# Low halves of the weights made on VectorE where norms run, in one step of a hybrid streaming encoder

## The chip, the core and the metric

The kernel runs on one core of one Trainium2 chip. The metric is the time of the program on the device in microseconds (us), the median of several runs. Besides the time there is a profile of one execution. The engines are called as in the profile: PE is TensorE (matmuls; PEld its weight loads), DVE is VectorE, ACT is ScalarE, POOL is GpSimd, SP is SyncE, which here issues the loads.

## What is computed

One layer of an encoder, for 512 tokens of a new stream and 8 x 16 tokens of running streams, 640 tokens of width 1024 in all, kept as five tiles of 128 tokens (tile 4 is the running streams). Cut to what matters:

```python
def encoder_layer(x, lw, ..., mem_k, mem_v):
    h = rmsnorm(x, lw['norm_mix'])
    a_qkv, b_qkv, b_beta, b_dec, b_gate, c_z, c_xbc, c_dt, gates = split_cols(h @ lw['w_in'], IN_SPLITS)
    ...
    m = ga * (ya @ lw['w_br_a']) + gb * (yb @ lw['w_br_b']) + gc * (yc @ lw['w_br_c'])
    x = x + m @ lw['w_out']
    x = x + memory_attn(rmsnorm(x, lw['norm_x']), mem_k, mem_v, lw['wx_q'], lw['wx_o'])
    hf = rmsnorm(x, lw['norm_ffn'])
    u, gf = jnp.split(hf @ lw['w_up'], 2, axis=-1)
    gf, f_conv_new = causal_dwconv(gf, f_conv, lw['f_conv_w'], lw['f_conv_b'])
    x = x + (u * jax.nn.silu(gf)) @ lw['w_down']
    return x, (...)

def memory_kv(mem, g, wk, wv):          # 256 memory rows, for the new stream
    m = rmsnorm(mem, g)
    return (m @ wk).reshape(...), (m @ wv).reshape(...)
```

`ya`, `yb` and `yc` come from three token mixers (chunk-band attention, gated DeltaNet, Mamba-2) that stand between the first projection and `w_out`; the change touches none of them.

## The kernel before

All matmuls are in a split float form. Each operand is held as a high half and a low half, both of type fp32r, and a product is three matmuls: high x high, low x high, high x low. For the activations a helper `split` (L258) makes the pair: ACT copies the value into the high half (line L250 of the profile), and another engine subtracts the high half from the value to get the low half (`tt`, L244). For weights `split_w` (L305) does the same on a block of 128 x 512 elements:

```python
            self.act(h[:, :m, :], x)
            eng = engs[b // half] if engs else self.nc.gpsimd
            ins = self.tt(l[:, :m, :], x, h[:, :m, :].bitcast(F32), ALU.subtract, eng)
```

So a low half of weights is made on POOL unless `engs` names an engine for the first and the second block of a loaded buffer. In the profile these instructions are `wl<-raw,wh` at L244, on POOL or on DVE. `raw` (L299) loads 512 KB of weights on the SP queue into one of 2 buffers, which are free again when both blocks' lows are made; high and low blocks have `NW = 6` buffers each, free again when PE has used them.

The work of the program is an in-order list for each engine. Which instruction stands where in a list is set by a scheduler when the program is built, from the order of the code and its own estimates; at run time an engine takes its list from the top, and an instruction that waits holds up all that stand behind it on its engine.

The norms are made in a chain that crosses the engines (`norm_T`, L519). ACT sums the squares of a token tile (`junk`); DVE turns the sums into a scale by some 14 tiny instructions of 128x1 or 128x2 elements (`inv_rms`, L487: names `v`, `y`, `w`, `t`); DVE multiplies the tile by scale and gain (`xn`, two instructions of 128x512 for each token tile, L247); PE transposes `xn` into PSUM (`nps`, L241); ACT copies the high half from there (`xTh`, `cTh`, `fTh`, `mTh`), and DVE makes the low half (`xTl` and so on). PE then multiplies these by weights.

Four stages run such chains while weights are split:

- **The front** (from 0 to some 45 us): tile 0, then tiles 1 and 2, then 3 and 4 are normed, and the attention values `V` (`tm`) are multiplied with four blocks of `w_in` from `rawv` and four from `raw`. The lows of the four `rawv` blocks are made at L1851 on POOL.
- **`w_out`** (955 to 1010 us): `add_proj` (L1520, called at L1933) goes through the 1024 columns in quarters of 256. A quarter loads two buffers, splits them in four blocks, and multiplies token tiles in pairs (0,1), (2,3), (4) (`ap<-wh,mh`); DVE adds the sums to `x`. All 16 lows are made on POOL. Between the quarters the norm of the memory (`mem_norm`, L1541) is run, two tiles of 128 rows (`mx`, `mT`).
- **Memory keys and values** (1010 to 1080 us): `mem_kv` (L1576) multiplies the normed memory by `wx_k` and `wx_v`, 8 steps of 256 columns with two buffers each (`tm<-wh,mTh`), woven with the norm of `x` for the cross attention (`cT`). Of the 32 lows, 16 are made on POOL and 16 on DVE.
- **The output of the cross attention** (1257 to 1298 us): `wx_o` is applied in the units `WP` (tiles 0 to 3, three quarters, earlier), `WL` (L1980: last quarter, all tiles) and `WS` (L1981: tile 4, three quarters). `WL` and `WS` split 16 blocks, 8 on POOL and 8 on DVE (`both`, L1962). The norm of the feed-forward (`fT`) runs beside them: tiles 0 and 1, tiles 2 and 3, and tile 4 when `WS` is done; then the feed-forward starts (`fps`, `ups`), whose lows are made on POOL.

Of the kernel before, what the change touches and what calls it, by code (L numbers as in the profile page):

```python
# [18 lines left out]
NK = 8  # L19
# [16 lines left out]
QUARTERS = ((0, 256), (256, 256), (512, 256), (768, 256))  # L36
# [9 lines left out]
class Enc:  # L46
# [1190 lines left out]
    def gates(self, X, gcol, tgs, mts):  # L1237
        w = self.I["w_in"][0]
        for mt in mts:
            def run(ps):  # L1240
                tg = tgs[mt] = self.U("tg")
                self.act(tg.rearrange("p (a b) -> p a b", a=2), ps[:, :, :HALF], AF.Tanh, scale=0.5)
            yield from self.fmj(lambda: self.weights(w, gcol + mt * P, P, 0, NK), X, run, nm="gps")

    def branch(self, X, Y, wbr, gcol, tgs, first):

        ahead = max(len(tgs), 1)
        yield from self.gates(X, gcol, tgs, range(len(tgs), ahead))
        Y = Y()
        nk = len(Y)  # L1250
        for mt in range(NK):
            yield from self.gates(X, gcol, tgs, range(mt + ahead, min(mt + ahead + 1, NK)))

            def run(ps):
                tg = tgs.pop(mt)
                tv = tg.rearrange("p (a b) -> p a b", a=2)
                self.stt(tv, tv, 1.0, ps[:, :, :HALF], ALU.add, ALU.mult)
                if first:
                    self.m.append(tg)
                else:  # L1260
                    self.tt(self.m[mt], self.m[mt], tg, ALU.add)
            if nk == 8:
                wk, c = (lambda: self.weights(wbr, mt * P, P, 0, 8)), 0
            else:
                if mt % 2 == 0:
                    pair = self.weights(wbr, mt * P, 256, 0, nk)
                wk, c = pair, (mt % 2) * P
            yield from self.fmj(wk, Y, run, c=c, nm="pps")
# [307 lines left out]
    def mem_kv(self):  # L1576
        I, O = self.I, self.O
        res = []
        for name, w in (("mem_k_prompt", I["wx_k"][0]), ("mem_v_prompt", I["wx_v"][0])):
            T = [[self.U("mkv", shape=(P, 512)) for _ in range(2)] for _ in range(2)]  # L1580
            res.append(T)
            dst = O[name][0, 0].rearrange("s h d -> s (h d)")
            for c in range(4):
                def cb(pair, ps):
                    for j, t in enumerate(pair):
                        self.act(T[t][c // 2][:, (c % 2) * 256:(c % 2) * 256 + 256], ps[:, j, :256])
                        if c % 2:
                            x = T[t][c // 2]
                            self.store(dst[t * P:(t + 1) * P, (c // 2) * 512:(c // 2 + 1) * 512], x)
                            if name == "mem_v_prompt":  # L1590
                                T[t][c // 2] = [self.U("mv", F32R, (P, 512)) for _ in range(2)]
                                self.split(*T[t][c // 2], x, self.nc.gpsimd)
                yield from self.tmj(lambda: self.weights(w, c * 256, 256, 0, NK, (self.nc.gpsimd, self.nc.vector)), self.MX, cb, tiles=range(2))
            if w is I["wx_v"]:
                break
            if len(res) == 1:
                K = T
                self.KT = []
        for h in range(4):
            pt = self.PP("mkt")  # L1600
            for dd in range(2):
                f = 2 * h + dd
                for kt in range(2):
                    self.tr(pt[:, dd * 256 + kt * P:dd * 256 + (kt + 1) * P],
                            K[kt][f // 4][:, (f % 4) * P:(f % 4 + 1) * P])
            o = [self.U("mKT", F32R, (P, 512)) for _ in range(2)]
            self.split(*o, pt)
            self.KT.append(o)
        self.MV = res[1]
# [211 lines left out]
    def run(self):  # L1821
        I = self.I
# [3 lines left out]
        w = I["w_in"][0]  # L1826
# [15 lines left out]
        for c, t in ((0, 1), (1, 3)):  # L1842
            if c == 0:
                tile0 = self.last_act
                for a in range(2):
                    wv += self.split_w(raws[a], 2, 512, loose=True)
            else:
                with self.tc.issue_after(tile0.ins):
                    for r in rawv:
                        h, l = (self.wp.tile([P, 512], F32R, name=self.nm("w" + b), tag="w" + b) for b in "hl")  # L1850
                        self.split(h, l, r, self.nc.gpsimd)  # L1851
                        wv.append((h, l))
            all_(self.norm_T(x0, g, X, ((t, t + 1),)))
        X = X[1]
# [69 lines left out]
        M = []  # L1924
        for mt in range(NK):
            h, l = self.U("mh", F32R), self.U("ml", F32R)
            self.act(h, self.m[mt], scale=0.5)
            self.stt(l, self.m[mt], 0.5, h.bitcast(F32), ALU.mult, ALU.subtract)
            M.append((h, l))
        x = [self.load_x(t) for t in range(NT)]  # L1930
        mem = self.mem_norm()
        next(mem)
        for i, _ in enumerate(self.add_proj(I["w_out"][0], M, x, cols=QUARTERS)):  # L1933
            if i % 10 == 9:
                next(mem, None)
        all_(mem)
# [4 lines left out]
        _, X = to  # L1941
# [16 lines left out]
        _, OX = self.XT("ox")  # L1958
        OS = [[self.U("os" + a, F32R, (P, 4, P)) for _ in range(2)] for a in "hl"]
        OS = [(OS[0][k // 4][:, k % 4, :], OS[1][k // 4][:, k % 4, :]) for k in range(NK)]  # L1960
        S = {}
        both = (self.nc.gpsimd, self.nc.vector)  # L1962
        self.add("WP", self.add_proj(I["wx_o"][0], OX, x, tiles=range(4), cols=QUARTERS[:3]), after=("XP",))
        cur = None
        for i in range(12):
# [19 lines left out]
        _, X = to  # L1985
# [53 lines left out]
```

## Time and profile before

| what | before |
|---|---|
| time, median of 3 runs | 1771.53 us (1765.14, 1771.53, 1771.67) |
| the profiled execution's own time | 1764.74 us |
| its span, first to last instruction | 1763.0 us |
| mean granted clock of TensorE, share of full speed | 0.985 |
| chain that ended last, PE's and DVE's shares | 69% and 11% of the span |
| moved by DMA | 181.78 MB, mean 103 GB/s |

The profiled execution took 1.7 us beyond its span, and 6.8 us less than the median of the runs. A row of the timeline reads: start, duration, engine, line, operation, output<-inputs, shapes, count, and in brackets how long the engine was idle before it and what ended that. Where a row has a count above one, the duration is that of the whole run of instructions.

### The profile page before, as it was taken

How to read it: one execution, taken by the hardware profiler on the slowest of the kernel's cores; microseconds unless marked ns; L12 is line 12 of the kernel's file. 1: busy time of each engine (PE TensorE's matmuls, PEld its weight loads, DVE VectorE, ACT ScalarE, POOL GpSimd, SP SyncE). 2: the span in 40 equal slices, each digit the busy share in tenths (PEclk: the TensorE clock that was granted, in tenths of full speed). 3: DMA queues.
4: the chain of work that ended last, by engine and by line, in shares of the span. 5: the costliest groups of instructions: out<-in, count | busy, mean ns of one | idle time of the engine just before them, and what ended most of it. 6: DMA issues, size and time to landing. Idle time of an engine off the chain costs nothing.

```text
span 1763.0 us, 32520 instructions
## 1 busy us (share of the span) xinstructions
PE 1678.3 (95%) x12953; PEld 1539.4 (87%) x12953; DVE 867.3 (49%) x1762; ACT 650.0 (37%) x1596; POOL 610.2 (35%) x641
## 2 busy tenths in 40 slices
PE   7999999999999998999999899999889999999997
PEld 5887778898988898998899899987689989998996
DVE  6155762437777764756434472243564404431443
ACT  4234544324443432443342354342443313331332
POOL 3342221123332343453432335211143433433432
PEclk8999999999999999999999999999999999999999
DMA  6322166222232334335323345146332222222221
GB/s 191 100 74 61 43 197 209 93 82 79 54 81 77 98 108 114 86 101 145 85 61 119 109 131 179 49 168 239 121 96 78 80 72 78 79 73 79 77 86 72
DMA packets 232830, 181.78 MB, mean 103 GB/s; under 512 B 14401, under 2 KB 198726, under 8 KB 232550
## 3 DMA queue, kind: packets, MB, share of 16 engines
q1 hardware_dynamic: 210752, 165.74, 30.8%
q10 hardware_dynamic: 21926, 13.96, 2.6%
q8 instruction: 102, 1.67, 0.4%
q14 instruction: 50, 0.41, 0.1%
HBM read 163.09 MB, written 16.06 MB: 102 GB/s over the span
## 4 chain that ended last, share of the span: by engine, by line
PE 69%; DVE 11%; ACT 3%; DMA 3%; issue 2%; POOL 1%; ACTq 0%; SPq 0%; POOLq 0%; DVEq 0%
PE ups L236 9%; PE fps L236 9%; PE dn L236 8%; PE gps L236 8%; PE pps L236 6%; PE ap L236 5%; PE tm L236 5%; PE qps L236 3%; PE cps L236 2%; DVE xc L247 2%; PE bps L236 2%; PE pl L236 1%; DVE t L244 1%; PE py L236 1%; PE t5a L241 1%
## 5 line engine op out<-in xcount | busy, mean ns | idle before, releaser
L244 POOL TENSOR_TENSOR wl<-raw,wh 128x512 fp32r<-128x512 f32 x369 | 489.2, 1330 | 940.6 <-ACT wh L250 770.9
L250 ACT ACTIVATE wh<-raw 128x512 fp32r<-128x512 f32 x396 | 246.5, 629 | 567.5 <-PE fps L236 92.9
L247 DVE SCALAR_TENSOR_TENSOR xc<-xp,vec,xc 128x664 f32<-128x664 f32 (+1 forms) x116 | 117.3, 1011 | 3.2
L236 PE MATMUL gps<-xTh,wh 128*128 128x320 f32 x448 | 116.3, 338 | 0.0
L236 PE MATMUL gps<-xTh,wl 128*128 128x320 f32 x448 | 106.2, 315 | 0.0
L236 PE MATMUL gps<-xTl,wh 128*128 128x320 f32 x448 | 105.3, 314 | 0.0
L569 DVE TENSOR_SCALAR xc<-xp,vec 128x656 f32<-128x656 f32 (+1 forms) x34 | 32.9, 966 | 130.0 <-ACT xp L250 130.0
L236 PE MATMUL dn<-wh,hh 128*128 128x512 f32 x220 | 86.1, 392 | 0.2 <-DVE x L244 0.2
L236 PE MATMUL dn<-wl,hh 128*128 128x512 f32 x220 | 85.8, 390 | 0.0
L236 PE MATMUL dn<-wh,hl 128*128 128x512 f32 x220 | 85.7, 390 | 0.0
L236 PEld LDWEIGHTS gps<-xTh,wh 128*128 128x128 f32 x448 | 73.4, 191 | 11.2 <-issue 10.6
L236 PE MATMUL fps<-fTh,wh 128*128 128x320 f32 x352 | 82.1, 311 | 0.0
L236 PE MATMUL ups<-fTh,wl 128*128 128x320 f32 x352 | 82.1, 311 | 0.0
L236 PE MATMUL ups<-fTl,wh 128*128 128x320 f32 x352 | 82.0, 311 | 0.0
L236 PE MATMUL ups<-fTh,wh 128*128 128x320 f32 x352 | 81.9, 310 | 0.0
L236 PE MATMUL fps<-fTh,wl 128*128 128x320 f32 x352 | 81.8, 310 | 0.0
L236 PE MATMUL fps<-fTl,wh 128*128 128x320 f32 x352 | 81.7, 310 | 0.0
L236 PEld LDWEIGHTS gps<-xTh,wl 128*128 128x128 f32 x448 | 75.5, 189 | 1.0 <-issue 0.8
L236 PEld LDWEIGHTS gps<-xTl,wh 128*128 128x128 f32 x448 | 75.3, 189 | 0.7 <-issue 0.6
L244 DVE TENSOR_TENSOR x<-x,dn 128x512 f32<-128x512 f32 x30 | 19.3, 684 | 104.9 <-PE dn L236 104.6
L236 PE MATMUL tm<-wh,xTh 128*128 128x256 f32 (+1 forms) x200 | 64.8, 324 | 4.6 <-ACT xTh L250 2.3
L236 PE MATMUL tm<-wl,xTh 128*128 128x256 f32 (+1 forms) x200 | 63.6, 318 | 1.1 <-POOL wl L244 1.1
(525 smaller groups left out, 4443.9 us busy)
## 6 DMA issues: line engine op xcount, KB each, us to landing
raw<-in_w_in_dram SPq DMA_DIRECT2D x70, 512.0 KB
raw<-in_w_up_dram SPq DMA_DIRECT2D x44, 512.0 KB
raw<-in_w_down_dram SPq DMA_DIRECT2D x22, 512.0 KB
ck<-in_cache_attn_k_dram SPq DMA_DIRECT2D x32, 256.0 KB
cv<-in_cache_attn_v_dram SPq DMA_DIRECT2D x32, 256.0 KB
xck<-in_cache_mem_k_dram SPq DMA_DIRECT2D x32, 256.0 KB
xcv<-in_cache_mem_v_dram SPq DMA_DIRECT2D x32, 256.0 KB
raw<-in_wx_o_dram SPq DMA_DIRECT2D x14, 512.0 KB
```

The source lines that it names most:

```text
L236: self.nc.tensor.matmul(out, lhsT=lhsT, rhs=rhs, start=start, stop=stop)
L241: self.nc.tensor.transpose(out, in_, self.ident[b:b + k, b:b + k])
L244: return (eng or self.nc.vector).tensor_tensor(out, a, b, op=op)
L247: self.nc.vector.scalar_tensor_tensor(out, a, s, b, op0=op0, op1=op1)
L250: self.last_act = self.nc.scalar.activation(out, in_, f, **kw)
L569: nc.vector.tensor_scalar(acc[:, :n], xp[:, :n], taps[0], bias, op0=ALU.mult, op1=ALU.add)
```

## The change

Four places now name VectorE for the lows. The first `split` has no engine argument any more, and `tt` takes VectorE then.

```diff
@@ mem_kv
-                yield from self.tmj(lambda: self.weights(w, c * 256, 256, 0, NK, (self.nc.gpsimd, self.nc.vector)), self.MX, cb, tiles=range(2))
+                yield from self.tmj(lambda: self.weights(w, c * 256, 256, 0, NK, (self.nc.vector, self.nc.vector)), self.MX, cb, tiles=range(2))
@@ run, the front
-                        self.split(h, l, r, self.nc.gpsimd)
+                        self.split(h, l, r)
@@ run, w_out
+        dve = (self.nc.vector, self.nc.vector)
         mem = self.mem_norm()
         next(mem)
-        for i, _ in enumerate(self.add_proj(I["w_out"][0], M, x, cols=QUARTERS)):
+        for i, _ in enumerate(self.add_proj(I["w_out"][0], M, x, cols=QUARTERS, engs=dve)):
@@ run, the cross attention's output (WL and WS)
-        both = (self.nc.gpsimd, self.nc.vector)
+        both = (self.nc.vector, self.nc.vector)
```

4 lows of the front, 16 of `w_out`, 16 of the memory's keys and values and 8 of `WL` and `WS` move: 44 in all. POOL's list gets 44 rows shorter (635 to 591) and DVE's 44 longer (1670 to 1714). No load, copy, matmul or sum is added or removed; the scheduler places some of them differently. Three places:

DVE's list in the front, at the scale of tiles 1 and 2 (`v`, `w`, `y`, `t`: the tiny instructions; `rawv`: the weights of `V`):

```order
 L501 TENSOR_SCALAR w_228<-v_227 128x2
 L500 TENSOR_SCALAR y_229<-y_229 128x2
+L244 TENSOR_TENSOR wl_282<-rawv_97,wh_281 128x512
 L244 TENSOR_TENSOR t_230<-y_229,w_228 128x2
+L244 TENSOR_TENSOR wl_286<-rawv_98,wh_285 128x512
 L244 TENSOR_TENSOR t_230<-t_230,y_229 128x2
+L244 TENSOR_TENSOR wl_290<-rawv_99,wh_289 128x512
 L247 SCALAR_TENSOR_TENSOR y_229<-t_230,y_229 128x2
+L244 TENSOR_TENSOR wl_294<-rawv_100,wh_293 128x512
```

The four lows now stand between the tiny instructions, ahead of the `xn` of these tiles. Further down the fourth `xn` of this group moves behind three `xTl`.

DVE's list in `w_out`, at the scale of the second memory tile (`xn_11583` is its first scaled half, `x_11259` a tile that gets a sum of `w_out`):

```order
+L244 TENSOR_TENSOR wl_11673<-raw_11670,wh_11672 128x512
 L244 TENSOR_TENSOR t_11568<-y_11567,w_11566 128x1
+L244 TENSOR_TENSOR wl_11677<-raw_11670,wh_11676 128x512
+L244 TENSOR_TENSOR t_11568<-t_11568,y_11567 128x1
+L244 TENSOR_TENSOR wl_11820<-raw_11817,wh_11819 128x512
+L247 SCALAR_TENSOR_TENSOR y_11567<-t_11568,y_11567 128x1
+L244 TENSOR_TENSOR x_11259<-x_11259,ap_11625 128x256
+L244 TENSOR_TENSOR t_11568<-y_11567,w_11566 128x1
+L244 TENSOR_TENSOR wl_11824<-raw_11817,wh_11823 128x512
 L244 TENSOR_TENSOR t_11568<-t_11568,y_11567 128x1
 L247 SCALAR_TENSOR_TENSOR y_11567<-t_11568,y_11567 128x1
 L247 SCALAR_TENSOR_TENSOR xn_11583<-mx_11556,y_11567,grow_11263 128x512
```

Four lows and one sum now stand in this chain. PE's list at the transpose of that half (`nps_11650`), before:

```order
L236 MATMUL ap_11625<-wh_11488,ml_11240 128x256
L236 MATMUL ap_11625<-wl_11489,mh_11239 128x256
L241 MATMUL nps_11650<-ident,xn_11583 128x128 x4
L236 MATMUL ap_11680<-wh_11662,mh_11211 128x256
L236 MATMUL ap_11680<-wh_11662,ml_11212 128x256
```

and now:

```order
L236 MATMUL ap_11680<-wl_11677,mh_11235 128x256
L236 MATMUL ap_11680<-wh_11676,mh_11239 128x256
L236 MATMUL ap_11680<-wh_11676,ml_11240 128x256
L241 MATMUL nps_11650<-ident,xn_11583 128x128 x4
L236 MATMUL ap_11680<-wl_11677,mh_11239 128x256
L236 MATMUL ap_11680<-wh_11662,mh_11211 128x256
```

The transpose stood ahead of all matmuls of `ap_11680`, the next pair of tiles, and now stands behind 23 of them. In the first memory tile likewise `nps_11390` stands 4 matmuls later.

DVE's list in the output of the cross attention, at the end of the scale of tiles 2 and 3 (`xn_15010` is their first scaled half, `raw_14956` the last buffer of `wx_o`), before:

```order
L247 SCALAR_TENSOR_TENSOR y_14859<-t_14860,y_14859 128x2
L247 SCALAR_TENSOR_TENSOR xn_15010<-x_11251,y_14859,grow_14778 128x512
L247 SCALAR_TENSOR_TENSOR xn_15019<-x_11253,y_14859,grow_14780 128x512
L244 TENSOR_TENSOR wl_14963<-raw_14956,wh_14962 128x512
L247 SCALAR_TENSOR_TENSOR xn_15028<-x_11255,y_14859,grow_14778 128x512
```

and now:

```order
L244 TENSOR_TENSOR wl_14959<-raw_14956,wh_14958 128x512
L244 TENSOR_TENSOR t_14860<-t_14860,y_14859 128x2
L244 TENSOR_TENSOR wl_14963<-raw_14956,wh_14962 128x512
L247 SCALAR_TENSOR_TENSOR y_14859<-t_14860,y_14859 128x2
L244 TENSOR_TENSOR fTl_14776<-nps_14975,fTh_14774 128x4x128
L244 TENSOR_TENSOR fTl_14777<-nps_14996,fTh_14775 128x4x128
L244 TENSOR_TENSOR x_11261<-x_11261,ap_14966 128x256
L247 SCALAR_TENSOR_TENSOR xn_15010<-x_11251,y_14859,grow_14778 128x512
```

Both lows of the last buffer now stand ahead of the `xn` of tiles 2 and 3; before, one was on POOL and one stood behind two of the four `xn`.

## Rows read from the trace of the kernel before

**Rows 1.** Page, part 1: busy us, share of the span, instructions.

```profile
PE 1678.3 (95%) x12953; PEld 1539.4 (87%) x12953; DVE 867.3 (49%) x1762; ACT 650.0 (37%) x1596; POOL 610.2 (35%) x641
```

**Rows 2.** The instructions on tile xn: who waited for them (us, times).

```profile
  PE nps L241: 20.3, 10
```

**Rows 3.** Lows of weights on DVE: duration ns min/median/max, first and last start.

```profile
L244 DVE TENSOR_TENSOR wl<-raw,wh x27: 678/854/1760, 1011.9 to 1723.7; 128x512 fp32r<-128x512 f32 x27
```

**Rows 4.** Timeline of the front (tiles 1 and 2).

```profile
17.39 0.16 DVE L244 TENSOR_TENSOR v<-ss 128x2 f32<-128x2 f32 x1 [3.33 <-ACT junk L250]
...
17.95 5.00 POOL L244 TENSOR_TENSOR wl<-rawv,wh 128x512 fp32r<-128x512 f32 x4 [2.42 <-ACT wh L250]
...
17.99 1.27 DVE L500 TENSOR_SCALAR y<-y 128x2 int32<-128x2 int32 x1
...
21.12 1.15 ACT L250 ACTIVATE wh<-raw 128x512 fp32r<-128x512 f32 x2 [1.69 <-DMA raw<-in_w_in_dram]
...
22.91 2.48 POOL L244 TENSOR_TENSOR wl<-raw,wh 128x512 fp32r<-128x512 f32 x2
...
24.22 1.19 DVE L244 TENSOR_TENSOR t<-t,y 128x2 f32<-128x2 f32 x1
...
26.23 2.74 DVE L247 SCALAR_TENSOR_TENSOR xn<-x,y,grow 128x512 f32<-128x512 f32 x4
...
27.03 1.97 PE L241 MATMUL nps<-ident,xn 128*128 128x128 f32 x8 [4.30 <-DVE xn L247]
```

**Rows 5.** Timeline of w_out, first memory tile.

```profile
972.46 5.06 POOL L244 TENSOR_TENSOR wl<-raw,wh 128x512 fp32r<-128x512 f32 x4 [12.06 <-ACT wh L250]
...
976.32 1.21 DVE L244 TENSOR_TENSOR v<-ss 128x1 f32<-128x1 f32 x1 [1.92 <-ACT junk L250]
...
980.69 1.11 PE L241 MATMUL nps<-ident,xn 128*128 128x128 f32 x4 [1.95 <-DVE xn L247]
```

**Rows 6.** Windows: stretch, its us, busy (count) by engine, PEclk, DMA share, GB/s.

```profile
980.00:985.00 5.00, 4.31 (x24) 4.31 (x25) 2.71 (x6) 2.54 (x8) 0.00 (x0) 0.66 0.36 128
...
955.00:1010.00 55.00, 49.51 (x392) 48.90 (x391) 23.93 (x58) 13.58 (x31) 13.28 (x11) 0.97 0.43 143
...
1257.00:1298.00 41.00, 29.34 (x190) 26.16 (x190) 34.88 (x83) 22.68 (x55) 15.77 (x11) 0.92 0.34 103
```

**Rows 7.** Timeline of w_out, second memory tile.

```profile
990.74 2.80 ACT L250 ACTIVATE wh<-raw 128x512 fp32r<-128x512 f32 x4 [5.95 <-issue]
...
991.60 1.16 DVE L244 TENSOR_TENSOR t<-t,y 128x1 f32<-128x1 f32 x1
...
994.01 3.40 DVE L247 SCALAR_TENSOR_TENSOR xn<-mx,y,grow 128x512 f32<-128x512 f32 x2
...
995.78 0.66 PE L241 MATMUL nps<-ident,xn 128*128 128x128 f32 x4 [2.86 <-DVE xn L247]
```

**Rows 8.** Waits of PE, 950 to 1100 us: us in total, times, longest.

```profile
PE nps L241 <- DVE xn L247: 8.6, 4, 2.9
```

**Rows 9.** Groups on DVE, 1010 to 1080 us: count | busy us, mean ns | idle before.

```profile
L244 DVE TENSOR_TENSOR wl<-raw,wh 128x512 fp32r<-128x512 f32 x16 | 17.9, 1120 | 13.9 <-ACT wh L250 13.6 <-issue 0.3
```

**Rows 10.** Timeline of the cross attention's output.

```profile
1264.38 0.69 DVE L244 TENSOR_TENSOR wl<-raw,wh 128x512 fp32r<-128x512 f32 x1
1264.99 1.25 DVE L244 TENSOR_TENSOR t<-y,w 128x2 f32<-128x2 f32 x1
...
1269.93 1.24 DVE L498 TENSOR_SCALAR v<-v 128x2 f32<-128x2 f32 x1
...
1271.89 1.78 DVE L247 SCALAR_TENSOR_TENSOR xn<-x,y,grow 128x512 f32<-128x512 f32 x1
...
1278.56 1.15 ACT L250 ACTIVATE wh<-raw 128x512 fp32r<-128x512 f32 x2 [3.54 <-DMA raw<-in_wx_o_dram]
...
1278.78 2.43 DVE L247 SCALAR_TENSOR_TENSOR xn<-x,y,grow 128x512 f32<-128x512 f32 x2
...
1294.27 0.69 PE L241 MATMUL nps<-ident,xn 128*128 128x128 f32 x4 [3.89 <-DVE xn L247]
```

## The prediction

> **What bounds the kernel now.** I read the page first: PE is busy 95% of the span [rows 1], so nothing else can be worth much unless PE waits for it. Then I asked who waits for the norms. PE waited ten times, 20.3 us in all, for an `xn` to transpose [rows 2]; that is about a quarter of all the time PE is not busy (1763.0 less 1678.3 is 85 us), and more than this sum an edit of the norms can hardly win, apart from what the clock does.
>
> Then the timeline around these waits. In the front, the reader should compare tiny DVE instructions: the first takes 0.16 us; six in the chain, from 17.99 to 24.22, take 1.18 to 1.27 us each, 7.25 us together [rows 4]. POOL makes its lows over just that time, 5.00 us for four and then 2.48 for two, some 1.25 each [rows 4]. Six lows, six long instructions: while POOL makes a low, the DVE instruction that stands next is held until that low ends. The lows on DVE show the same from the other side: 0.68 us at least, 1.76 at most [rows 3]. So a norm that runs beside POOL's lows has its chain stretched by about 1.05 us a low, and PE waits at its end.
>
> **The parts.** Nothing is taken out or added; 44 lows move. A low costs DVE 0.61 us of its list (start to next start, 1264.38 to 1264.99, [rows 10]) and gives back up to 1.05 us where it held a DVE instruction. POOL gets 44 times 1.25, 55 us, less; nobody waits longer for what stays on it. On SP one load of `wx_k` moves ahead of two gain vectors; the `xn` that read those come 30 us later, so I count nothing. Buffers of raw weights come free some 0.6 us sooner, since a low is 0.68 in place of 1.25 us; I count nothing for that either.
>
> *Front.* From `v` at 17.39 to the first `xn` at 26.23 is 8.84 us, of which the six long instructions hold 7.25 less 6 x 0.16, 6.3 us [rows 4]. Without holds 2.55 are left; the four moved lows add 4 x 0.61, 2.45: the `xn` would start at 22.4. But the two lows of the next weights stay on POOL and start sooner than 22.91: their highs begin at 21.12 [rows 4], so the first comes at about 21.7. Each may hold one instruction of DVE for 1.05. So the first `xn` starts between 22.4 and 24.5, a gain of 3.8 to 1.7. One of the two falls ahead of it, I think (2.8), and 0.3 I take off because the fourth `xn` now stands behind three other instructions: **2.5**. That PE ran at the lower clock after this wait I leave as it is.
>
> *`w_out`, first memory tile.* `v` takes 1.21 in place of 0.16 because POOL is at its four lows until 977.5 [rows 5]. In the new order the four lows come ahead of `v`, and can be done: their highs were there when POOL made its own, and DVE needs 4 x 0.61, 2.4 us from 972.5. So `xn` comes 1.05 sooner; and 4 matmuls now go ahead of the transpose, at 49.51/392, 0.13 us each [rows 6], 0.5. The wait of 1.95 [rows 5] falls to 0.4: **1.5**. Right behind that wait the granted clock is 0.66 on average over 980 to 985 [rows 6], so two thirds of that stretch, 3.4 us, were at 1.2 in place of 2.4 GHz, which is 1.7 us of PE's work. The engine had idled just before. I take it that with a wait of 0.4 the clock stays up: **1.7**; at worst nothing, since the fall may come at another wait.
>
> *`w_out`, second memory tile.* PE waits 2.86 [rows 7]. Now 23 matmuls, 2.9 us, stand ahead of the transpose, and their lows are ready by 993. The chain loses its holds (1.16 and 3.40 us, where 0.16 and two `xn` of 0.69 were due: 3.0 us, [rows 4, 7]) but has four lows in it, 2.45 us, the last of which needs a high that ends at 990.74 + 2.80, 993.5 [rows 7], and one sum. I put the `xn` at 995.5 and its transpose at 996.3 in place of 995.78, while PE works until 992.9 + 2.9: a wait of 0.6 is left: **2.2**. Cover: DVE is busy 23.9 of 55 us here [rows 6], so it has room for 16 lows, 9.8 us; were that room gone, each low would cost its 0.61. Bounds for the whole of `w_out`: 0.5 if the second chain slips by 2 us and the clock falls elsewhere, 6.5 if all of it goes.
>
> *Memory keys and values.* Of 8.6 us of waiting [rows 8] 3.8 belong here (8.6 less 1.95 and 2.86), at two transposes. The 16 lows DVE has already average 1.12 us where 0.68 is the least [rows 3, 9]: 7.0 us of holding, which goes with POOL's lows. The 16 new ones cost 9.8. As a sum DVE gets 2.8 us more to do, but ahead of the first late `xn` three new lows (1.8) take the place of holds of two lows and two or three tiny instructions (nearly 3), and the second no longer stands behind a low (0.7). I take **1.7**; at most 3.8, at worst -1.0.
>
> *Output of the cross attention.* DVE is the fullest here, 34.9 of 41 us [rows 6]. Four instructions are held by POOL's lows of `wx_o`, at 1264.99, 1269.93, 1271.89 and 1278.78 [rows 10]: 1.25, 1.24, 1.78 and 2.43 where 0.16, 0.17, 0.69 and 1.38 were due, 4.3 us. Four lows in this stretch add 2.4. But the `xn` of tiles 2 and 3 now wait for both lows of the last buffer, and POOL's lows for the feed-forward, which stay, will meet one more `xn` (1.05). I take **0.5**. At worst the last buffer lands as before, its highs run from 1278.56 to 1279.7 [rows 10], and the `xn` start at 1281.2 in place of 1278.78: -2.4. At best PE's last wait of 3.89 goes.
>
> The sum is 2.5 + 1.5 + 1.7 + 2.2 + 1.7 + 0.5 = 10.1 us. The profiled execution took 1764.7, so the sum by it is 1754.6. It was 6.8 us below the median of the runs, two of which lie at 1771.6 and one at 1765.1; the 10.1 off the median give **1761**, which is what I predict.
>
> **Rivals.** *DVE pays back what it wins.* Both engines' lows and tiny instructions still need the same engine or each other. Added: 44 x 0.61, 26.8 us on DVE. Removed: 6.3 in the front, 1.05 and 3.0 in `w_out`, 7.0 for lows in the memory stage, 4.3 in the last: 21.7 us. If what counts is how much DVE has to do before the norms, nothing is won, and the time stays at 1771.5, within the 5 us by which these two sums differ. For it: DVE is nearly full in the last stage. Against it: in `w_out` DVE idles more than half the time. This is also what the Trainium skill would have: "Perfetto Trace Analysis", section "Optimizing Scalar/DVE Operations", says that GpSimd and VectorE share a read port of SBUF, held as a lock, so moving operations between the two might not help. Of the lock the trace agrees, 1.2 us for an instruction of 0.16; whether moving helps no row here shows.
>
> *The lows hold the norms.* A low at the head of DVE's list waits for its high on ACT, which waits for a load or a buffer, and the norm behind it waits too; on POOL its own wait for the high held nobody in DVE's list. The lows DVE has now waited 13.6 us for highs, 0.85 each [rows 9]. 44 more make 37 us; if half of it fell ahead of an `xn`, 18.7 us would be lost against 10.1 won: 1780, slower. It decides from 12 of the 44 lows on (10.1/0.85). The place would be the memory stage and the last one, where ACT waited 3.54 us for a load [rows 10]. Against it: 16 lows stand so on DVE already, and PE's waits there are 3.8 us only.
>
> **How the numbers follow.** A measurement of this kernel tells 0.5%, 8.9 us, from no change. The forecast, a gain of 5.5 to 15 us, has 0.62, of which 0.50 lies above 8.9 and 0.12 below. The first rival has 0.30, the second 0.08, a quarter of it within 0.5%. So faster 0.50, same 0.44, slower 0.06. The range: 1765.1, the lower level of the runs, less 15 is 1750; at the other end no gain at the upper level, 1771. What lies beyond, the slower cases and half of a tail of the first rival, is less than 2 in 10.
>
> **What would show it.** In the front the tiny instructions between 17 and 23 us back at 0.16, and the transposes of tile 1 at 24.5 in place of 27.03. In `w_out` waits below 0.7 for both memory tiles, and no clock below 1 in the five microseconds behind the first. Lows on DVE at a median near 0.69 in place of 0.854 [rows 3]. PE's waits for `xn` at 10 to 13 us in place of 20.3. Wrong it would be if these waits shrink and new ones for a low on DVE take their place, if DVE is seen waiting for `wh` ahead of an `xn` by more than a microsecond in several places, or if the tile-4 transpose comes later after the start of its stage than now.

## The result, and the profile after

The changed kernel takes 1757.5 us (median of 6 runs, 1754.1 to 1760.9); the kernel before, on the same chip, 1770.5 (1765.1 to 1771.7). The ratio is 0.9933, 95% interval 0.9916 to 0.9949: by that ratio faster by 11.9 us, where 10.1 were forecast (the medians differ by 13.0). Measured again later, on another occasion, the ratio was 0.9927 (0.9911 to 0.9943).

The two profiled executions differ by less, 1763.0 and 1758.9 us of span, because the one before, at 1764.7 us, was faster than any of its runs, and the one after, at 1760.7, the second slowest of its own. So the spans decide nothing here, and the stages have to be read one by one.

Part 1 of the page of the changed kernel (busy us, share, instructions):

```profile
PE 1681.3 (96%) x12953; PEld 1542.2 (88%) x12953; DVE 866.2 (49%) x1806; ACT 651.4 (37%) x1596; POOL 550.3 (31%) x597
```

DVE has 44 instructions more than in [rows 1] and is busy no longer: 866.2 us, where it was 867.3. POOL is busy 59.9 us less, and what the new lows cost DVE it got back elsewhere. Where from, the lows show (instructions on the tile `wl`; min/median/max ns):

```profile
L244 DVE TENSOR_TENSOR wl<-raw,wh x67: 680/686/695, 945.5 to 1719.7; 128x512 fp32r<-128x512 f32 x67
```

In [rows 3] the median was 854 and the longest 1760; now not one of 67 is over 0.70 us. And who waits for an `xn` (instructions on that tile, us and times), against 20.3 and 10 in [rows 2]:

```profile
  PE nps L241: 12.6, 9
```

The timeline of the front shows the mechanism and its remainder:

```profile
17.66 0.16 DVE L244 TENSOR_TENSOR v<-ss 128x2 f32<-128x2 f32 x1 [3.33 <-ACT junk L250]
...
18.06 0.17 DVE L499 TENSOR_SCALAR y<-v 128x2 int32<-128x2 int32 x1
...
18.35 0.69 DVE L244 TENSOR_TENSOR wl<-rawv,wh 128x512 fp32r<-128x512 f32 x1
...
18.96 0.15 DVE L244 TENSOR_TENSOR t<-y,w 128x2 f32<-128x2 f32 x1
...
22.09 2.94 POOL L244 TENSOR_TENSOR wl<-raw,wh 128x512 fp32r<-128x512 f32 x2 [6.27 <-ACT wh L250]
22.14 4.09 DVE L247 SCALAR_TENSOR_TENSOR xn<-x,y,grow 128x512 f32<-128x512 f32 x3
...
23.95 0.66 PE L241 MATMUL nps<-ident,xn 128*128 128x128 f32 x4 [2.25 <-DVE xn L247]
...
38.80 0.59 ACT L250 ACTIVATE V<-tm 128x512 f32<-128x512 f32 x1
...
39.45 0.49 PE L236 MATMUL tm<-wh,xTh 128*128 128x512 f32 x1 [1.18 <-ACT V L250]
```

The tiny instructions are back at 0.15 to 0.17 us, each low costs DVE 0.61 (18.35 to 18.96), and tile 1 is transposed at 23.95 in place of 27.03 [rows 4]. The two lows that stayed on POOL still stretch three `xn` to 4.09 us, where three alone take 2.1. And a wait stands at 39.45 that was not there: an eviction of V now comes behind the third `xTh` of tiles 3 and 4 on ACT; before, it came behind the first.

Windows cut at the stages' ends in each run (stretch, us, busy and count of PE, PEld, DVE, ACT, POOL, PEclk, DMA share, GB/s): `w_out`, the memory's keys and values, the cross attention's output. Before:

```profile
958.00:1026.00 68.00, 62.51 (x506) 61.90 (x505) 29.22 (x78) 20.07 (x47) 17.32 (x13) 0.97 0.38 124
1026.00:1081.00 55.00, 50.62 (x423) 50.07 (x422) 34.96 (x64) 29.89 (x63) 25.00 (x18) 1.00 0.55 173
...
1258.00:1404.00 146.00, 134.75 (x904) 132.03 (x905) 83.83 (x143) 59.37 (x134) 61.63 (x66) 0.98 0.28 84
```

After:

```profile
962.00:1023.00 61.00, 60.04 (x498) 59.55 (x497) 30.16 (x91) 19.43 (x45) 0.00 (x0) 1.00 0.41 139
1023.00:1076.00 53.00, 52.18 (x433) 51.33 (x432) 34.71 (x79) 30.74 (x64) 4.06 (x4) 1.00 0.57 179
...
1253.00:1400.00 147.00, 137.11 (x905) 134.63 (x906) 81.77 (x149) 59.61 (x134) 53.80 (x61) 0.95 0.28 83
```

`w_out` loses 6 to 7 us and has the full clock throughout, the memory stage 2 to 3, with PE busy all but 0.8 us of it. The cross attention's output gains nothing here, at a lower mean clock (0.95, was 0.98). To the hundredth, from the first and last matmul of each stage, with the time in parentheses for which the trace has TensorE at 1.2 in place of 2.4 GHz, this table holds the profiled execution of every kernel of this study:

```
us (of it at 1.2 GHz)  front         middle         w_out        memory       cross out
before                56.90 (13.7)  901.53 (20.5)  67.24 (3.4)  55.41 (0.0)  146.93 ( 6.8)
after                 58.02 (13.7)  904.36 (23.9)  61.04 (0.0)  52.25 (0.0)  147.49 (13.7)
after_again           56.75 (13.7)  910.31 (37.5)  60.98 (0.0)  51.79 (0.0)  145.53 ( 6.8)
hold_all              60.41 (13.7)  905.11 (27.3)  67.56 (3.4)  59.57 (3.4)  147.47 ( 6.8)
no_front              57.05 (10.2)  903.01 (23.9)  60.97 (0.0)  51.53 (0.0)  146.09 ( 6.8)
front_pre             54.07 (10.2)  904.05 (23.9)  60.83 (0.0)  51.24 (0.0)  144.96 ( 6.8)
no_cross              59.91 (17.1)  904.19 (27.3)  60.83 (0.0)  51.56 (0.0)  147.17 (10.2)
wout_only             56.68 (13.7)  903.30 (27.3)  61.54 (0.0)  57.18 (3.4)  149.11 (13.7)
mem_only              56.98 (10.2)  902.87 (23.9)  67.11 (3.4)  51.64 (0.0)  146.79 (10.2)
more_front            53.91 (10.2)  903.50 (23.9)  60.83 (0.0)  52.39 (0.0)  146.17 (10.2)
more_ffn              53.76 ( 6.8)  900.80 (20.5)  60.87 (0.0)  51.81 (0.0)  143.82 (10.2)
more_ffn_again        53.39 (10.2)  906.16 (30.7)  60.85 (0.0)  51.57 (0.0)  141.09 ( 0.0)
more_both             53.93 ( 3.4)  906.52 (30.7)  61.15 (0.0)  51.62 (0.0)  141.49 ( 3.4)
```

Front: to the first query-key matmul. Middle: to the first matmul on the halves of m. `w_out`: to the last of these. Memory: to the last on the memory's tokens. Cross out: from the last matmul of the cross attention's values to the first of `w_down`. The rest (scores, and the feed-forward's end) is 176.5 to 179.4 and 358.4 to 358.8 us everywhere. One of the six runs of more_both took 4099 us and is left out of its median.

### The profile page after: what moved, and what is told of

Same layout as the page of the kernel before. It is cut to its first block, busy times and chain, and to the rows that moved or that the text cites. A ratio compares the mean times of both kernels' runs of the same rounds, so it can differ in the third digit from the quotient of the medians.

```text
span 1758.9 us, 32484 instructions
## 1 busy us (share of the span) xinstructions
PE 1681.3 (96%) x12953; PEld 1542.2 (88%) x12953; DVE 866.2 (49%) x1806; ACT 651.4 (37%) x1596; POOL 550.3 (31%) x597
## 4 chain that ended last, share of the span: by engine, by line
PE 68%; DVE 11%; DMA 4%; ACT 3%; issue 2%; POOL 0%; ACTq 0%; SPq 0%; POOLq 0%; DVEq 0%
PE ups L236 9%; PE fps L236 9%; PE dn L236 8%; PE gps L236 8%; PE pps L236 6%; PE ap L236 5%; PE tm L236 3%; PE qps L236 3%; DVE xc L247 2%; PE cps L236 2%; PE bps L236 2%; PE pl L236 1%; DMA raw<-in_wx_v_dram 1%; PE py L236 1%; PE xkt L241 1%
## 5 line engine op out<-in xcount | busy, mean ns | idle before, releaser
L244 POOL TENSOR_TENSOR wl<-raw,wh 128x512 fp32r<-128x512 f32 x329 | 433.7, 1322 | 871.9 <-ACT wh L250 788.9
L236 PE MATMUL tm<-wh,xTl 128*128 128x256 f32 (+1 forms) x200 | 63.6, 318 | 0.0
```

Of the source, the lines that this page charges most:

```text
L236: self.nc.tensor.matmul(out, lhsT=lhsT, rhs=rhs, start=start, stop=stop)
L244: return (eng or self.nc.vector).tensor_tensor(out, a, b, op=op)
```

## The experiments

All ratios are to the kernel before on the same chip, with 95% intervals.

**The hold alone.** Does POOL's pass hold DVE, or are the lows just ready sooner on DVE? The changed kernel, with a dummy pass on POOL for each moved low (hold_all):

```
+    def idle_low(self, h):
+        t = self.xpp.tile([P, 684], F32, ...)
+        self.tt(t[:, :512], h, h, ALU.subtract, self.nc.gpsimd)
```

> The changed kernel, in which POOL makes a subtraction of the same size (128x512, high minus high, into a tile that nobody reads) for each of the 44 lows that moved; the order on PE, ACT and SP is that of the changed kernel. Theory, POOL's pass holds DVE: the holds are back while DVE still has the 44 lows, so waits for xn are above 15 us again (12.6 in the changed kernel, 20.3 before), DVE lows have a mean of 0.85 us or more in place of 0.69, and the time is 1766 to 1778 us, 0.998 to 1.004 of before. Rival, the lows are merely ready sooner on DVE and free their buffers sooner: lows and waits as in the changed kernel, 1757.5 us, ratio 0.993.

1780.0 us, ratio 1.006 (1.0036 to 1.0084): all of the gain is gone and 11 us more, 2 us above the range expected. The timeline of the front shows the hold come back, pass by pass:

```profile
18.10 5.59 POOL L244 TENSOR_TENSOR idle<-wh 128x512 f32<-128x512 f32 x4 [2.38 <-ACT wh L250]
18.14 1.02 DVE L507 TENSOR_SCALAR y<-y 128x2 int32<-128x2 int32 x1
19.08 0.68 DVE L244 TENSOR_TENSOR wl<-rawv,wh 128x512 fp32r<-128x512 f32 x1
19.68 0.99 DVE L244 TENSOR_TENSOR t<-y,w 128x2 f32<-128x2 f32 x1
```

The tiny instructions take 1.0 us again, where they took 0.15 in the changed kernel. The instructions on `xn` (who waited) and part 1 of the page:

```profile
  PE nps L241: 20.2, 13
```

```profile
PE 1685.0 (95%) x12953; PEld 1543.9 (87%) x12953; DVE 893.1 (50%) x1806; ACT 651.0 (37%) x1596; POOL 608.2 (34%) x641
```

The waits of [rows 2] are back, at 20.2 us, though none of the 44 lows is made on POOL. DVE does the same 1806 instructions as in the changed kernel and takes 26.9 us longer for them, 0.61 for each of POOL's 44 passes. The groups on DVE from 960 to 1100 us (count, busy, mean) account for half of it: the lows themselves, 0.99 us each on average, 0.69 in the changed kernel.

```profile
L244 DVE TENSOR_TENSOR wl<-raw,wh 128x512 fp32r<-128x512 f32 x45 | 43.7, 991 | 10.7 <-ACT wh L250 9.4 <-PE tm L236 0.6 <-PE ap L236 0.6
```

By stages (table), the dummies cost 6.5 us in `w_out` and 7.3 in the memory stage (a fall of the clock, 1.7 us, in each), 2.4 in the front. The rival, lows merely ready sooner, is out: they were made by the same engine, in the same place of its order. Of DVE's list only two copies of 0.16 us stand elsewhere, at 1300 in place of 745 us. That the dummies hold up buffers or POOL's own work is out too: in the trace no instruction of another engine waits for one of them, and PE waits for no low of POOL. It is also the case that the forecast had no price for: lows on DVE with POOL still as busy beside them are worse than lows on POOL.

**One stage alone.** The kernel before with the edit in `w_out` only, and in the memory's keys and values only (wout_only, mem_only):

```
-add_proj(I["w_out"][0], M, x, cols=QUARTERS)
+add_proj(I["w_out"][0], M, x, cols=QUARTERS, engs=dve)
```

> The kernel before with only the 16 lows of w_out on VectorE. Theory, each stage's gain is its own: the stage of w_out (first to last matmul on the halves of m) takes 61.0 to 61.5 us as in the changed kernel, in place of 67.2, the memory stage behind it 55.3 to 55.6 as before, the time is 6 us below before, ratio 0.9965 (0.995 to 0.998). Rival, the w_out gain is partly a fall of the clock that moved (1.7 us of it): 62.5 to 63.5 us with a half-clock stretch inside it, ratio 0.9975.

```
-self.weights(w, c * 256, 256, 0, NK, (self.nc.gpsimd, self.nc.vector))
+self.weights(w, c * 256, 256, 0, NK, (self.nc.vector, self.nc.vector))
```

> The kernel before with only the 16 lows of the memory keys and values on VectorE. Theory, the stage from the last matmul on m to the last on the memory's tokens gives its 3.2 us by itself: 52.2 us in place of 55.4, ratio 0.998 (0.996 to 1.0). Rival, it wins only the 1.7 us that the prediction named, and the other 1.5 came from w_out's end being less crowded: 53.7 us, ratio 0.999.

`w_out` alone: 1764.7 us, 0.9975 (0.9965 to 0.9985). The stage takes 61.5 us, 5.7 less, as expected; but the memory stage behind it grew from 55.4 to 57.2, which neither theory had. Its waits (PE, 950 to 1095 us) and a window around one of them:

```profile
PE nps L241 <- DVE xn L247: 5.5, 3, 2.5
```

```profile
1030.00:1037.00 7.00, 4.49 (x26) 4.34 (x25) 5.13 (x9) 3.63 (x10) 1.27 (x1) 0.76 0.47 152
```

The clock, whole in `w_out` now, falls behind a wait of 2.5 us in the stage that follows (it ends at 1032.7): 3.4 us at half speed, 1.7 us lost. In this run that part of `w_out`'s gain, the clock's, was not kept, since the next long wait was still there.

The memory stage alone: 1766.3 us, 0.9978 (0.9966 to 0.9990). The stage takes 51.6 us, 3.8 less, so it wins the whole by itself, and more than the 3.2 of the theory. `w_out`, with its two waits as before, keeps its 3.4 us at half clock. The two kernels gain 0.25% and 0.22%, 0.47 of the 0.67 together. Of the 3.5 us that are left, the fall of the clock in wout_only is 1.7; the rest lies within the intervals.

**The front and the cross attention's output taken back.** The changed kernel with the front's four lows on POOL again, and with the cross attention's eight on both engines again (no_front, no_cross):

```
-self.split(h, l, r)
+self.split(h, l, r, self.nc.gpsimd)
```

> The changed kernel with the four lows of the front back on POOL. Theory, the front's gain of 3.1 us at tile 1's transposes is given back by the order that follows (fourth xn behind other work, eviction of V late): the first query-key matmul of the attention comes at 56.9 us as before, 1.1 sooner than in the changed kernel (58.0), and the time is that of the changed kernel or up to 1.5 us less, ratio 0.992 to 0.9935. Rival, the front gains its 2.5 us and only falls of the clock elsewhere hid it: the time is 2.5 us above the changed kernel's, 1760, ratio 0.9948.

```
-both = (self.nc.vector, self.nc.vector)
+both = (self.nc.gpsimd, self.nc.vector)
```

> The changed kernel with the eight lows of the last quarters of the cross attention's output weights shared between POOL and DVE as before. Theory, the part wins 3.9 us at the end of the sample tile's matmuls and the clock, at half for 13.6 us in place of 6.8, takes it back: from the last matmul of the cross attention's values to the first of w_down 147.0 us, as in the kernel before (146.9), and the time within 1 us of the changed kernel's. Rival, the lows on DVE delay the norm of the feed-forward (waits of 1.73 and 1.04 us that were not there): without them the stage is 1 to 2.5 us shorter than in either kernel, 144.5 to 146, ratio 0.9915 to 0.9925.

Without the front's edit: 1756.5 us, 0.9930 (0.9908 to 0.9953), the same as with it (1757.5 and 1757.3) within the noise. The front takes 57.05 us, and 58.02, 56.75 and 59.91 in three runs with the edit (after, after_again, no_cross). The first two differ by what comes ahead of the edit. The `v` of tiles 1 and 2 starts at 17.66 us in the changed kernel (its timeline above) and here, in its second run, at

```profile
16.32 0.16 DVE L244 TENSOR_TENSOR v<-ss 128x2 f32<-128x2 f32 x1 [3.33 <-ACT junk L250]
```

Counted from that `v` to the first query-key matmul, the front takes 39.5 us in all four kernels with the front as before (before, no_front, wout_only, mem_only), and 40.4 in both runs of the changed kernel (42.8 in no_cross, with 3.4 us more at half clock). So the edit of the front by itself loses 0.9 us, near the 1.1 of the order theory.

Without the cross attention's edit: 1761.0 us, 0.9951 (0.9937 to 0.9965). The stage takes 147.2 us, so the rival (shorter without the edit) is wrong, but the time is 3.5 above the changed kernel's, not within 1. In the profiled run part of this is the clock, which was at half for 17.1 us of the front. To compare the stage, half of the half-clock time is taken off, which is about what it costs while PE works (two runs of one middle, below: 13.6 us more at half clock, 5.9 us longer). So the stage is 143.5, 142.1, 142.3 and 141.7 where POOL makes half of these lows (before, this run, and the two of one stage alone), 142.4 in the mean, and 140.7, 142.1, 142.7, 141.6 and 141.1 (after, after_again, no_front, front_pre, more_front), 141.6, where DVE makes all. The edit is worth 0.8 us, less than the scatter of either group. The intervals of the two times overlap; how much of the 3.5 is the edit's stays open.

**Where the front's 3 us went.** The changed kernel, in which `norm_T` makes the four `xn` of a pair of tiles ahead of the rest, in the front only (front_pre):

```
+            if pre:
+                for i, t in enumerate(tiles):
+                    for j in range(2):
+                        xns.append(self.U("xn", shape=(P, 512)))
+                        self.stt(xns[-1], x[t][j][:, :512], r[:, i:i + 1], gain[j], ...)
```

> The changed kernel, in which the front makes all four xn of a pair of tiles ahead of the first xTl, as the order before had it; V's evictions come ahead of the third xTh again. Theory, the order gave the gain back: the first query-key matmul comes at 54 to 55.5 us (56.9 before, 58.0 in the changed kernel), no wait of PE for V's eviction above 0.5 us at 39 us, and the time is 2.5 to 4 us below the changed kernel's, ratio 0.991 to 0.992. Rival, the two lows of the next weights that stay on POOL hold the xn and that is what takes the gain: 57 to 58 us, ratio 0.993.

1755.2 us, 0.9917 (0.9890 to 0.9944); the front 54.07 us. Counted from the `v` it is 36.5, 3.9 less than the changed kernel's and 3.0 less than without the front's edit; the four later runs that keep this order have 36.4 to 36.9. Waits of PE in the first 62 us, changed kernel, then this one (us in total, times, longest):

```profile
PE nps L241 <- DVE xn L247: 6.2, 4, 2.4
PE tm L236 <- ACT xTh L250: 3.3, 2, 2.6
PE tm L236 <- ACT V L250: 1.9, 2, 1.2
```

```profile
PE nps L241 <- DVE xn L247: 6.6, 5, 2.3
PE tm L236 <- ACT xTh L250: 2.3, 1, 2.3
```

The waits for V are gone and one for `xTh`; those for `xn` remain. In this run the order of `xn`, `xTl`, `xTh` and V on both engines is that of the kernel before. So the moved lows did win their 3 us, and the new order of DVE and ACT, with the fourth `xn` behind three `xTl` and V's eviction behind a third `xTh`, lost them and 0.9 more. Which of the two cost how much was not taken apart.

**More of the same.** If POOL's passes are what holds, the lows next to other norms should move too: the two of the attention's first weights, and the four of the feed-forward's first two blocks. On top of front_pre, more_front has the one, more_ffn the other, more_both both.

```
 in attn_dense:
+self.weights(w, j * 512 + p * P, P, 0, NK, (self.nc.vector,) * 2 if p == j == 0 else None)
 in ffn, for gate and up:
+self.weights(wu, ..., P, 0, NK, (self.nc.vector,) * 2 if first else None)
```

> The kernel with the four xn of a pair made first, and the two lows of the attention's first weights, which POOL still made beside those xn, on VectorE too. Theory, POOL's passes hold DVE: the four xn take 2.7 us in place of 4.75, the two lows cost DVE 1.2 us ahead of them, the first query-key matmul comes 0.5 to 1.5 us sooner (52.6 to 53.6 us in place of 54.1), ratio 0.991 to 0.9915. Rival, each low has its price on DVE whatever POOL does: 0.5 to 1.5 us later, 54.6 to 55.6 us, ratio 0.992 to 0.9925.

> The kernel with the four xn of a pair made first, and the four lows of the feed-forward's first two blocks of weights, which POOL made beside that norm's last xn, on VectorE too. Theory, POOL's passes hold DVE: the waits of 1.74 and 1.04 us at the last tiles' transposes and of 2.9 at tile 4's shrink by 1 to 2.5 us together, the stage from the last matmul of the cross attention's values to the first of w_down takes 143 to 144 us in place of 145.0, ratio 0.9905 to 0.9915. Rival, DVE is too full there (34.9 of 41 us before) and each low shifts the xTl and xn behind it: 145.5 to 147 us, ratio 0.992 to 0.993.

> All of these edits together: the changed kernel, the four xn of a pair made first, and on VectorE also the two lows of the attention's first weights and the four of the feed-forward's first two blocks. Theory, POOL's passes hold DVE, and the front is by now bound by its own chain: the feed-forward's part adds its 7 us to a front that stands where it stood (53.9 us for the first query-key matmul), 1747 us, ratio 0.9865 to 0.9885. Rival, part of the 7 us were falls of the clock that this run happened to lack, and the half-clock time is what differs: 1750 to 1753 us, ratio 0.9895 to 0.991.

The front: 1753.7 us, 0.9912 (0.9899 to 0.9925), the stage 53.91 in place of 54.07, so neither theory. The timeline of front_pre, then of this kernel:

```profile
22.04 4.75 DVE L247 SCALAR_TENSOR_TENSOR xn<-x,y,grow 128x512 f32<-128x512 f32 x4
...
23.84 0.66 PE L241 MATMUL nps<-ident,xn 128*128 128x128 f32 x4 [2.26 <-DVE xn L247]
...
25.61 2.79 PE L241 MATMUL nps<-ident,xn 128*128 128x128 f32 x12 [1.11 <-DVE xn L247]
```

```profile
21.61 0.69 DVE L244 TENSOR_TENSOR wl<-raw,wh 128x512 fp32r<-128x512 f32 x1 [1.08 <-ACT wh L250]
...
23.66 2.74 DVE L247 SCALAR_TENSOR_TENSOR xn<-x,y,grow 128x512 f32<-128x512 f32 x4
...
24.47 3.68 PE L241 MATMUL nps<-ident,xn 128*128 128x128 f32 x16 [3.39 <-DVE xn L247]
```

The four `xn` take 2.74 as expected, 2.0 less, and start 1.6 later (2.1 counted from the `v`): two lows stand ahead of them, and the first waits 1.08 us for its high. This is the forecast's second rival in small, the low that holds the norm, and it just eats what the hold gave.

The feed-forward: 1748.0 us, 0.9883 (0.9870 to 0.9897), better than expected; the stage 143.8, inside the expected range. Both together, though: 1752.3 us, 0.9904 (0.9883 to 0.9924). Here the rival was right, that some of the 7 us were the clock's: the last stage kept its gain (141.5), but the middle, which no edit touches, took 906.5 us in place of 900.8, with 30.7 us at half clock in place of 20.5.

**The same kernels again**, side by side, to see what is the clock's:

> The changed kernel once more, beside the next one on the same chip. Theory, what differs between runs of one kernel is where the clock falls to half in the middle of the program, which the change does not touch: the stages keep their lengths (w_out 61.0, memory 52.2 us), the middle (first query-key matmul to first on the halves of m, 904.4 us) moves by up to 5 us with its half-clock stretches, ratio 0.9925 to 0.9945. Rival, the stages themselves scatter by 1 us or more between runs.

> The fastest kernel so far (the four xn of a pair made first, the four lows of the feed-forward's first blocks on VectorE) once more, beside the changed kernel. Theory, its 9.5 us over the changed kernel are 2.5 to 3 of the front, 2 of the feed-forward's norm and the rest falls of the clock: 5 to 8 us below the changed kernel, ratio to before 0.988 to 0.991. Rival, all of it is the edits': 9 us or more again, ratio 0.987 to 0.9885.

1757.3 us, 0.9927 (0.9911 to 0.9943), and 1749.9 us, 0.9885 (0.9869 to 0.9901): 7.4 us between them on one chip, inside the 5 to 8 of the theory. `w_out` and memory stage of the changed kernel repeat to 0.5 us. The front moved by 1.3, all of it ahead of the `v`, and the cross attention's output by 2.0, with 6.9 us less at half clock, so for these two the rival is right. The middle moved most, 904.4 and 910.3, and the 13.6 us more at half clock account for it (6.8 of time against 5.9). Window of the middle, first and second run of the changed kernel:

```profile
58.00:962.00 904.00, 864.59 (x7561) 789.11 (x7560) 514.60 (x1109) 352.85 (x948) 307.32 (x339) 0.99 0.33 97
```

```profile
57.00:967.00 910.00, 870.50 (x7562) 793.60 (x7561) 513.74 (x1109) 352.52 (x948) 306.55 (x339) 0.98 0.33 96
```

The same matmuls, 5.9 us more of PE's busy time, and a lower clock. The kernel with the `xn` first and the feed-forward's four lows on DVE beats both kernels: 1748.0 and 1749.9 us, some 20 below the kernel before. Waits of PE for `xn` in the last stage (1245 to 1300 us), the changed kernel, then the second run of this one:

```profile
PE nps L241 <- DVE xn L247: 5.0, 3, 2.3
```

```profile
PE nps L241 <- DVE xn L247: 1.9, 2, 1.6
```

## Why the prediction was right

The value forecast, 1761, is 3.5 us above the measured 1757.5, inside the range, and faster by more than 0.5% had the largest chance. The mechanism was the right one: POOL's passes hold DVE's short instructions and with them the norms, and hold_all brings the hold back without moving a low. That the sum comes so near is in part luck, since a front that was priced too high and a memory stage that was priced too low make up for each other. Term by term:

- *Front, 2.5*: the transposes came 3.1 us sooner (23.95; 24.5 was forecast). As time the term measured -0.9. The step that failed is to count a gain at one wait as a gain of the stage: the forecast took 0.3 off for the fourth `xn` behind three other instructions, and did not look at ACT, where V's eviction had moved behind a third `xTh`.
- *`w_out`, 1.5 + 1.7 + 2.2 = 5.4*: measured 6.2 and 5.7. The first wait fell from 1.95 [rows 5] to 0.96 (0.4 forecast), the second from 2.86 [rows 7] to nothing (0.6 forecast), so the sign of waits below 0.7 came for the second alone. The clock, 0.66 in [rows 6], stayed up around the first:

```profile
980.00:985.00 5.00, 4.04 (x35) 3.84 (x34) 3.78 (x17) 0.94 (x3) 0.00 (x0) 1.00 0.58 198
```

- *Memory keys and values, 1.7*: 3.0 to 4.2 in the runs that have its edit without dummies. The term was undersized. Of the 3.8 us of waits that it named nearly all went, as the changed kernel's waits of PE from 950 to 1100 us show, for [rows 8] (1.0 of the 1.4 is the first memory tile of `w_out`):

```profile
PE nps L241 <- DVE xn L247: 1.4, 2, 1.0
```

The groups of DVE from 1010 to 1080 us, for [rows 9], have the cost as forecast: 15 more lows make 2.6 us more of busy time.

```profile
L244 DVE TENSOR_TENSOR wl<-raw,wh 128x512 fp32r<-128x512 f32 x31 | 20.5, 688 | 12.4 <-ACT wh L250 12.3
```

The lows do stand in the norms' chains. At the first late transpose five of them stand between the `v` and the `xn` in place of three, and the chain is 1.2 us shorter, as forecast. At the second the forecast counted 0.7, for one low that no longer stands ahead of the `xn`. Its chain lost more, the hold of a low and a wait for a high among it, and took 10.10 us in place of 12.21. Before:

```profile
1038.92 0.14 DVE L244 TENSOR_TENSOR v<-ss 128x1 f32<-128x1 f32 x1
...
1040.47 1.76 DVE L244 TENSOR_TENSOR wl<-raw,wh 128x512 fp32r<-128x512 f32 x1
...
1047.76 1.36 DVE L244 TENSOR_TENSOR wl<-raw,wh 128x512 fp32r<-128x512 f32 x1 [1.09 <-ACT wh L250]
...
1051.13 2.07 DVE L247 SCALAR_TENSOR_TENSOR xn<-x,y,grow 128x512 f32<-128x512 f32 x3
```

After:

```profile
1034.78 0.15 DVE L244 TENSOR_TENSOR v<-ss 128x1 f32<-128x1 f32 x1
...
1044.88 1.41 DVE L247 SCALAR_TENSOR_TENSOR xn<-x,y,grow 128x512 f32<-128x512 f32 x2
```

- *Cross attention's output, 0.5*: about 0.8 with the clock taken out, less than the runs scatter. Its sign of being wrong did come: tile 4's transpose is 37.5 us behind the last value matmul (1252.9 to 1290.4), 36.7 before. PE has two new waits of 1.73 and 1.04 us for `xn`, and one of 1.78 for a low, and the clock was at half for 13.7 us. Much of this belongs to POOL's lows for the feed-forward, which the forecast had priced at 1.05: with four of them on DVE the waits for `xn` fell from 5.0 to 1.9 us, and the stage to 141.1 to 143.8.

In the order of the list the terms as measured make -0.9 + 6.2 + 3.5 + 0.8, some 9.6 us, of 11.9. The interval of the ratio reaches from 9.0 to 14.9 us, so the rest is not told from noise; the middle alone lies between 900.8 and 910.3 us in these runs without any edit to it.

The rival that had 0.30, DVE pays back what it wins, was nearly right as a balance of work (866.2 against 867.3 us) and wrong about time. What counts is how long the chains ahead of an `xn` take, and these got shorter though lows stand in them. The Trainium skill says in "Perfetto Trace Analysis", section "Optimizing Scalar/DVE Operations", that moving operations between GpSimd and VectorE might not help because they share a port. Here it did help, by 0.67%, at unchanged busy time of DVE. The rival of the lows that hold the norms came in small, in more_front; in the changed kernel it cost less than the holds had.

## What to carry over

Where a chain of short instructions on VectorE bounds TensorE, look for GpSimd passes beside it: the chain's tiny instructions show 1.2 us in place of 0.16, and taking GpSimd's work over cost VectorE here no more than it had been held for (866.2 us busy in place of 867.3), but only because GpSimd then fell silent (893.1 with the dummies). Compare the order on the engines behind the mended wait before counting its gain, ScalarE's evictions above all. And compare stage by stage, from a start behind whatever moves by itself, with the half-clock time beside each, since a stretch that nobody touched moved by 5.9 us between two runs of one kernel, half of this gain.

## What was not expected of the hardware

- The hold works both ways. In hold_all a dummy pass of 128x512 on POOL takes 1.04 us at the least; the median is 1.48 and the longest 2.15 (instructions on the dummy tile). The timeline shows one of 1.48, which starts 0.11 us after a low of DVE; the second low of the pair is then stretched in turn, two lows taking 2.14 us where 1.29 is usual. The longest started just behind the first of two lows. The Trainium skill, "SBUF — State Buffer", section "SBUF: two separate sides", has it that the shared port goes to whichever of the two starts first, for its whole instruction (on VectorE's side for instructions with two inputs from SBUF or in a two-port mode). The passes and the lows, each stretched by the other, agree with that.

```profile
L244 POOL TENSOR_TENSOR idle<-wh x44: 1035/1480/2154, 18.1 to 1288.6; 128x512 f32<-128x512 f32 x44
```

```profile
1083.70 2.14 DVE L244 TENSOR_TENSOR wl<-raw,wh 128x512 fp32r<-128x512 f32 x2 [3.44 <-ACT wh L250]
1083.81 1.48 POOL L244 TENSOR_TENSOR idle<-wh 128x512 f32<-128x512 f32 x1 [0.47 <-ACT wh L250]
```

- In `w_out` and the memory stage the falls of the clock came with PE's waits, and moved with them. With the edit in `w_out` alone the fall behind a wait of 1.95 us went, and one came behind a wait of 2.5 us in the next stage (wout_only). Both stages kept the full clock in all nine profiled executions with both edits and no dummies. Not every such wait brings a fall, though: in the kernel before those of 2.86 and 2.22 us had none. The middle of one and the same kernel had 23.9 and 37.5 us at half clock in two runs. What decides between these cases was not tried.
